# Another beginning, another end of the output projection and another entry of the feed-forward part in a one-core hybrid decoder layer

## The chip, the cores and the metric

The kernel runs on one core of a Trainium2 chip. A core has five engines that work side by side, each through its own list of instructions in order: PE (TensorE, matrix products), DVE (VectorE), ACT (ScalarE), POOL (GpSimd) and SP (SyncE, which here only starts transfers). An instruction waits on semaphores until its inputs are there and its output buffer is free; whatever stands behind it on its engine waits too. Matrix products read SBUF and write PSUM. The metric is the time in microseconds (us) of one execution on the device, taken as the median of several runs.

## The reference, cut to what matters

One decoder layer works on 512 prompt rows and 8 sample rows, 520 columns in all once the activations are transposed:

```python
sh1, sc1, g1, sh2, sc2, g2 = ada_mod(c, w_ada, b_ada)         # silu(c) @ w_ada + b_ada, six vectors
h = modulate(rmsnorm(x, norm1_w), sh1, sc1)                   # rmsnorm(x) * (1 + sc1) + sh1
mq, mk, ..., ga, gb = jnp.split(h @ w_in + b_in, SPLIT_POINTS, axis=-1)
...
merged = jax.nn.sigmoid(ga) * (y_m @ w_proj_a) + jax.nn.sigmoid(gb) * (y_f @ w_proj_b)
x = x + g1 * (merged @ w_out)
h2 = modulate(rmsnorm(x, norm2_w), sh2, sc2)
f_out, conv_new = conv_ffn(h2, conv_state, w_ffn_in, conv_w, conv_b, w_ffn_out)
x = x + g2 * f_out
```

`D_MODEL` is 2048, `D_FF` 5632, everything is float32. Between `split` and `merged` stand a matrix memory and an attention, which the change does not touch.

## The kernel before, in words

**Products.** Every float32 product is made of three products of a faster type: a weight tile is cast to `wh` on ACT and its remainder `wl` is formed on DVE; an activation is split in the same way into a high and a low part; PE forms `wh`·high, `wh`·low and `wl`·high. 2048 rows of activations are 16 chunks of 128 rows (`KC` = 16), the 520 columns are two halves `z` of 260 (`HN`). Weights come in raw tiles of 512 KB through SP; there are eight raw buffers, two sets of `wh`/`wl`, and a third one (`cf`) from the output projection on.

**The beginning.** The class `First` computes the first layer's shift and scale for two chunks at a time (a phase; `phases` has eight): it loads pieces of `w_ada` of 256 KB (`ar`), PE multiplies them (`adp`), ACT copies the sums (`ads`), PE transposes them (`adq`), DVE adds the bias (`ada`). Then the two chunks are modulated (`x`), split (`hh`, `hl`), and multiplied with two chunks' worth of eleven outputs of `w_in` (`NPRE`, tiles `pre`); the partial sums of the eleven outputs are kept, so that each phase adds to them. `load_group` loads these weights, in groups of four, four and three outputs. In the text the groups are numbered from g0, so g3 is the first group of phase 1. `next_group`, at outputs 1, 4 and 8 of a phase, loads one further group and splits the next one. At two visits per phase, `v0` and `v1`, PE does the next phase's `adp` products; at `v1 + 1` the next phase's `finish` and modulation follow. PSUM has two buffers for `pre`, so output j waits until the copy or the addition of output j − 2 is done. From the first phase on PE, DVE and ACT work in the order in which the code is written (`Ordered`).

**The output projection.** `merged @ w_out` runs as eight units (`WoPair`, two chunks of output each) of seven products, in the manner of Strassen; `run_pairs` gives each product a slot t (56 in all), and before it issues the preparations for later ones: `total` (sums of weight tiles), `split`, and `take`, which moves a finished product out of PSUM. The first unit has the order `ORDER1`, the others `ORDER`. A dictionary `late` hangs further work on single slots. Each finished output row chunk is stored (`dx2`), squared, added up for the next norm (by a transfer that accumulates on POOL), scaled and stored (`dxa`), except for the last pair, whose chunks are squared here and enter the norm directly (`half_squares`, `half_norm`).

**The entry of the feed-forward part.** `half_norm(z)` sums the squares on PE (`ms`) and `rsqrt` turns them into the factor of the norm (`rr`) on ACT and DVE. `features` makes the split activations (`bf`) of eight chunks and one half from the scaled rows `xa`. PE uses them at once: `fa`, `fg` and `fb` are the accumulators of the first columns; `beside` runs several weights over one set of activations, `eight` one weight. `cast` and `low` prepare `wh` and `wl`. Afterwards the regular units (`FfnPair`) begin.

Of the kernel before, what the change touches and what calls it, by code (L numbers as in the profile page):

```python
# [63 lines left out]
def tile_hybrid_step(ctx: ExitStack, tc: tile.TileContext, I, O):  # L64
# [191 lines left out]
    class Pair:  # L256
# [82 lines left out]
    def run_pairs(units, early, late, start=None):  # L339
        loads = {2: {1: ((0, 0),), 2: ((1, 0), (1, 1)), 5: ((0, 1),)},  # L340
                 1: {1: ((0, 0),), 3: ((1, 0), (1, 1)), 5: ((0, 1),)}}[early]
        for t in range(-early if start is None else start, 7 * len(units) + 5):
            u, r = divmod(t, 7)
            now, nxt = (units[v] if 0 <= v < len(units) else None for v in (u, u + 1))
            if 0 <= u - 1 < len(units):
                units[u - 1].after(r + 7)
            if now:
                if r > 0:
                    now.take(now.order[r - 1])
                now.ahead(r)  # L350
            if nxt:
                if r in loads and now:
                    nxt.load(*loads[r])
                if r >= 7 - early:
                    nxt.ahead(r - 7)
            if t in late:
                late[t]()
            if now:
                now.product(now.order[r])
# [92 lines left out]
    class First:  # L452
# [42 lines left out]

        def finish(self, c0, n):
            t = ada_turn(ada_out(self.ps, n), n)
# [10 lines left out]
        def steps(self, c0, n):  # L508
            return [lambda s=s: self.part(c0, n, s) for s in range(KC // 2)] + [lambda: self.finish(c0, n)]
# [31 lines left out]
    def modulate_first(u, c, eng):  # L541

        a, b = SC1 * 16 + c, SH1 * 16 + c
        V.tensor_scalar(u[:, :SEQ], u[:, :SEQ], ada[:, a, 0:1], ada[:, b, 0:1], op0=ALU.mult, op1=ALU.add)
        V.tensor_tensor(u[:, SEQ:N], u[:, SEQ:N], ada[:, a, 1:9], op=ALU.mult)
        V.tensor_tensor(u[:, SEQ:N], u[:, SEQ:N], ada[:, b, 1:9], op=ALU.add)
        return split(hp, "hl", u, "h", eng=eng)

# [24 lines left out]

    load_group()
    first.load(NPH)
    for _ in range(3):
        load_group()
# [7 lines left out]
    w_first = wtwo([raws.pop(0)[0]], m * NPH * P)  # L585
    h = []
# [7 lines left out]
    def first_chunks(c0, n):  # L594
        for c in range(c0, c0 + n):
            h.append(modulate_first(xs[c], c, V))

    normed(*phases[0])
    first.finish(*phases[0])
    first_chunks(*phases[0])  # L600
# [27 lines left out]
    T, V, S = (Ordered(tc, e) for e in (T, V, S))  # L628
    for i, (c0, n) in enumerate(phases):
        todo = {1: [next_group], 4: [next_group], 8: [next_group]}  # L630
        visits, steps = {}, []
        if i + 1 < len(phases):
            a, b = range(c0 + n, c0 + 2 * n)
            steps = first.steps(c0 + n, n)
            v0, v1 = {0: (3, 7), 1: (3, 6)}.get(i, (1, 4))
            visits = {v0: 4, v1: 4}
            for j, f, c in ((0, norm_x, a), (2, norm_x, b), (v1 + 1, mod_x, a), (v1 + 2, mod_x, b), (9, mod_low, a),
                            (10, mod_low, b)):
                todo.setdefault(j, []).append(on(f, c))
            todo[v1 + 1].append(on(mod_high, a))  # L640
            todo[v1 + 2].append(on(mod_high, b))
        for j in range(NPRE):
# [11 lines left out]
            for k in range(n):  # L654
                o = (j % m * n + k) * P
                for e, (a, b) in enumerate(((wh, h[c0 + k][0]), (wh, h[c0 + k][1]), (wl, h[c0 + k][0]))):
                    for z in range(2):
                        T.matmul(acc[:, z, :HN], a[:, o:o + P], b[:, z * HN:(z + 1) * HN],
                                 start=(k == 0 and e == 0), stop=(k == n - 1 and e == 2))
# [8 lines left out]
    xs = wh = wl = None  # L668
# [943 lines left out]
    class WoPair(AddPair):  # L1612
# [9 lines left out]
        def ahead(self, r):  # L1622
            super().ahead(r)
            if r == 0:
                self.fetch(lambda c: I["xT"][:, c, :])

        def done(self, e):
# [3 lines left out]
            if c == KC - 2 + e:  # L1631
                return
# [15 lines left out]
        def after(self, r):  # L1648
            if r > 8 or self.c == KC - 2:
                return  # L1650
            if r == 7:
                self.add(1, 0, self.x)
                self.done(0)
# [4 lines left out]
        def end(self, step):  # L1658

            if step == 0:  # L1660
                self.add(1, 0, self.x)
            if step == 1:
                super().c11()
                self.done(0)
                self.done(1)
# [86 lines left out]
    W2 = units[-1]  # L1752
# [11 lines left out]
    def half_squares(z):  # L1764
        a, b = z * HN, (z + 1) * HN
        if z:
            W2.sq = [pt("sq") for _ in range(2)]
        for e in range(2):
            S.activation(W2.sq[e][:, a:b], W2.x2[e][:, a:b], AF.Square)
# [10 lines left out]

    def first_weights(o):
        ws.append(parts2(0, o, 0))
        load2(1, o, 0)

    r2 = st("rr")
    run_pairs(units, 2, {
        0: lambda: (m_sums(7, 0), m_sums(7, 1), m_parts(7, 6)), 1: lambda: (m_parts(7, 5), m_sums(7, 2)),
# [564 lines left out]
```

## Time and profile before

| what | value |
|---|---|
| time, median of 3 runs | 2893.94 us (2893.7 to 2894.21) |
| the profiled execution's own time | 2878.36 us |
| its span in the trace | 2876.6 us |
| PE busy | 2836.9 us, 99% |
| weight loads (overlap PE) | 2728.6 us |
| DVE busy | 2153.9 us, 75% |
| ACT busy | 1367.4 us, 48% |
| POOL busy | 361.3 us, 13% |
| mean granted TensorE clock | 0.999 |
| bytes moved | 514.16 MB, mean 179 GB/s |

Read it thus: PE is busy nearly throughout, so a change of order can only win time where PE stands idle; and the other engines count where PE waits for them. The profiled execution is 15.6 us shorter than the median of the runs, so differences found in the profile are carried over to the median as differences. The rows themselves stand in the prediction.

### The profile page before, as it was taken

How to read it: one execution, taken by the hardware profiler on the slowest of the kernel's cores; microseconds unless marked ns; L12 is line 12 of the kernel's file. 1: busy time of each engine (PE TensorE's matmuls, PEld its weight loads, DVE VectorE, ACT ScalarE, POOL GpSimd, SP SyncE). 2: the span in 40 equal slices, each digit the busy share in tenths (PEclk: the TensorE clock that was granted, in tenths of full speed). 3: DMA queues.
4: the chain of work that ended last, by engine and by line, in shares of the span. 5: the costliest groups of instructions: out<-in, count | busy, mean ns of one | idle time of the engine just before them, and what ended most of it. 6: DMA issues, size and time to landing. Idle time of an engine off the chain costs nothing.

```text
span 2876.6 us, 58533 instructions
## 1 busy us (share of the span) xinstructions
PE 2836.9 (99%) x23460; PEld 2728.6 (95%) x23460; DVE 2153.9 (75%) x3992; ACT 1367.4 (48%) x2395; POOL 361.3 (13%) x649
## 2 busy tenths in 40 slices
PE   6999999999999999999999999999999999999999
PEld 4889998999998889899999999999999999999999
DVE  5777755677864566468888888888888887787787
ACT  4235643455554555334555444444454445544543
POOL 0001111211110112502211000000000001100100
PEclk9999999999999999999999999999999999999999
DMA  9934448844546576757763444444443436746752
GB/s 336 315 124 124 147 138 285 272 162 149 170 140 227 189 252 228 261 184 228 218 212 97 129 142 140 145 136 152 139 147 118 145 113 201 191 154 187 205 159 89
DMA packets 214138, 514.16 MB, mean 179 GB/s; under 512 B 24480, under 2 KB 77072, under 8 KB 213864
## 3 DMA queue, kind: packets, MB, share of 16 engines
q1 hardware_dynamic: 177072, 416.01, 45.0%
q0 software_dynamic: 36352, 94.18, 10.9%
q8 instruction: 184, 3.01, 0.4%
q14 instruction: 90, 0.74, 0.1%
q10 hardware_dynamic: 440, 0.23, 0.0%
HBM read 440.40 MB, written 66.46 MB: 176 GB/s over the span
## 4 chain that ended last, share of the span: by engine, by line
PE 85%; DVE 5%; issue 4%; DMA 3%; ACT 2%; POOL 0%; SPq 0%; ACTq 0%; POOLq 0%; DVEq 0%
PE x L60 31%; PE y L60 15%; PE z L60 8%; PE fi L223 7%; PE pre L60 4%; PE pa L223 3%; PE fo L60 3%; PE gate L223 3%; PE mo L223 2%; PE adp L428 2%; PE adp L60 1%; PE mv L223 1%; DMA ar<-in_w_ada 1%; DVE wl L60 1%; PE mk L223 1%
## 5 line engine op out<-in xcount | busy, mean ns | idle before, releaser
L60 ACT CAST wh<-sw 128x512 fp32r<-128x512 f32 x638 | 365.7, 621 | 245.6 <-PE z L60 75.8
L60 DVE TENSOR_TENSOR wl<-sw,wh 128x512 fp32r<-128x512 f32 x638 | 411.3, 686 | 87.0 <-ACT wh L60 84.2
L60 PE MATMUL x<-bf,wh 128*128 128x260 f32 x2624 | 476.2, 282 | 0.2 <-DVE tg L60 0.2
L60 ACT CAST wh<-raw 128x1024 fp32r<-128x1024 f32 (+2 forms) x349 | 315.7, 917 | 327.6 <-PE x L60 130.7
L60 DVE TENSOR_TENSOR wl<-raw,wh 128x1024 fp32r<-128x1024 f32 (+2 forms) x349 | 364.9, 1057 | 121.9 <-ACT wh L60 113.8
L60 PEld LDWEIGHTS x<-bf,wh 128*128 128x128 f32 x2624 | 403.4, 188 | 0.4 <-issue 0.4
L60 PE MATMUL x<-bf,wl 128*128 128x260 f32 x1312 | 369.6, 282 | 0.0
L178 DVE TENSOR_TENSOR wl<-raw,wh 128x1024 fp32r<-128x1024 f32 (+1 forms) x116 | 140.7, 1213 | 194.5 <-ACT wh L177 192.5
L60 PEld LDWEIGHTS x<-bf,wl 128*128 128x128 f32 x1312 | 247.0, 188 | 0.0
L60 PE MATMUL y<-bf,wh 128*128 128x260 f32 x1312 | 238.6, 282 | 0.0
L177 ACT CAST wh<-raw 128x1024 fp32r<-128x1024 f32 (+1 forms) x116 | 120.5, 1039 | 204.1 <-issue 46.6
L60 DVE TENSOR_TENSOR sw<-raw,raw 128x512 f32<-128x512 f32 x316 | 203.0, 683 | 0.0
L60 PEld LDWEIGHTS y<-bf,wh 128*128 128x128 f32 x1312 | 201.7, 188 | 0.0
L60 PE MATMUL x<-ff,wh 128*128 128x260 f32 x1024 | 185.9, 282 | 0.0
L60 PE MATMUL y<-bf,wl 128*128 128x260 f32 x656 | 184.8, 282 | 0.0
L60 PEld LDWEIGHTS x<-ff,wh 128*128 128x128 f32 x1024 | 157.6, 188 | 0.0
L60 PE MATMUL x<-ff,wl 128*128 128x260 f32 x512 | 144.5, 282 | 0.0
L60 PE MATMUL x<-hf,wh 128*128 128x260 f32 x720 | 131.0, 282 | 0.0
L60 PE MATMUL fo<-fe,wh 128*128 128x260 f32 x768 | 125.6, 284 | 1.2 <-DVE fo L60 1.1
L60 PEld LDWEIGHTS y<-bf,wl 128*128 128x128 f32 x656 | 123.5, 188 | 0.0
L60 PE MATMUL z<-bf,wh 128*128 128x260 f32 x656 | 120.6, 284 | 0.0
L60 PEld LDWEIGHTS x<-hf,wh 128*128 128x128 f32 x720 | 110.6, 188 | 0.0
(620 smaller groups left out, 7543.8 us busy)
## 6 DMA issues: line engine op xcount, KB each, us to landing
raw<-in_w_fi SPq DMA_DIRECT2D x176, 512.0 KB, 4.4
raw<-in_w_in SPq DMA_DIRECT2D x156, 512.0 KB, 4.6
ar<-in_w_ada SPq DMA_DIRECT2D x192, 256.0 KB, 6.3
raw<-in_w_ada SPq DMA_DIRECT2D x96, 512.0 KB, 4.2
raw<-in_w_fo SPq DMA_DIRECT2D x64, 512.0 KB, 4.0
raw<-in_w_out SPq DMA_DIRECT2D x32, 512.0 KB, 4.7
raw<-in_w_fo SPq DMA_DIRECT2D x32, 384.0 KB, 3.7
dff<-cc POOLq DMA_DIRECT2D x44, 260.0 KB, 4.3
```

Source lines behind the costliest of these rows:

```text
L60: return lambda *a, **k: self.tc.keep_in_program_order(getattr(self.eng, op)(*a, **k))
L177: S.copy(wh[:, o], t[:, :m])
L178: V.tensor_tensor(wl[:, o], t[:, :m], wh[:, o].bitcast(F32), op=ALU.subtract)
L223: T.matmul(acc[:, z, :HN], a[:, o], b[:, z * HN:(z + 1) * HN], start=(k == 0 and i == 0), stop=(k == K - 1 and i == 2))
L428: ins = T.matmul(ps[32 * g:32 * g + 32, :], cs[:, k, :], w, start=first, stop=last, tile_position=(0, 32 * g))
```

## The change: what it does

It has four parts.

1. *Beginning.* The loads start in another order: first all of phase 0's `ar`, then g0 and g1, four pairs of phase 1's `ar`, g2, then the remaining `ar` as far as buffers allow. g3 is no longer loaded ahead but by the first `next_group`. The first two chunks' high parts are written by ACT straight from `x` with scale and shift; DVE forms the modulated value afterwards for the low part. The first weight is split in two pieces, and phase 0's products are ordered by kind. The copy of the `adp` sums (`sums`) is separated from `finish` and done one output earlier. In phase 0 `v0` is 4 instead of 3. Modulation and high parts of both next chunks stand ahead of `next_group`.
2. *First unit of the output projection.* `m_parts(7, 6)` moves from slot 0 to slot 1, and there the split of the next weight comes ahead of `total(3)`.
3. *Last two units.* `run_pairs` takes a table of places; with `tail` the last two units share slots 40 to 55: their long products come one unit after the other, then the next-to-last unit's last two, then the last unit's last two. The last two pairs (four chunks) are no longer squared, accumulated and stored by transfers; all four are squared into tiles of their own for the norm, so that `half_norm` has four products with `ones` instead of two. Half of the norm and the first four features stand in slots 52 to 55.
4. *Entry.* The norm of the other half comes after all eight features instead of after four, one weight's products over half 0 are merged with those of two others, the scaling of the last rows moves, and `sums_of` lets a weight's `wl` be formed ahead of its last step.

On SP the loads of the beginning before stand thus (`ar` are pieces of `w_ada`, `raw` a group of `w_in`; the fourth `raw` of the program, raw38, is g3):

```order
L478 DMA ar35_182<-in_w_ada 128x2x256
L570 DMA raw36_184<-in_w_in 128x4x256
L570 DMA raw37_186<-in_w_in 128x3x256
L570 DMA raw38_188<-in_w_in 128x4x256
L478 DMA ar39_190<-in_w_ada 128x2x256
```

And after, further down the same queue, behind g0, g1, g2, all `ar` of phase 1 and part of phase 2's (raw100 is g3):

```order
L492 DMA ar94_370<-in_w_ada 128x2x256
L492 DMA ar95_372<-in_w_ada 128x2x256
L579 DMA raw100_394<-in_w_in 128x4x256
L492 DMA ar110_463<-in_w_ada 128x2x256
L492 DMA ar111_465<-in_w_ada 128x2x256
```

g3 was row 37 of SP, ahead of phase 1's `ar`, and is now row 63, in the place that g4 had (row 64).

On ACT at the end of phase 0 before (ads132 are the sums of phase 1, wh135 is the cast of g3, hh137 and hh143 are phase 1's high parts, the `pre` are copies of outputs 8 to 10):

```order
L60 COPY ads132_565<-adp106_427 128x256
L60 CAST wh135_578<-raw38_188 128x1024
L60 CAST hh137_585<-x4_91 128x520
L60 COPY pre140_601<-pre139_588 128x520
L60 CAST hh143_611<-x5_93 128x520
L60 COPY pre146_627<-pre145_614 128x520
L60 COPY pre148_643<-pre147_630 128x520
```

And after (hh135 and hh137 are the high parts, wh140 the cast of g3, pre143 the copy of output 8):

```order
L60 COPY ads125_542<-adp109_446 128x256
L60 COPY pre133_569<-pre132_556 128x520
L60 CAST hh135_583<-x4_91 128x520
L60 CAST hh137_589<-x5_93 128x520
L60 CAST wh140_594<-raw100_394 128x1024
L60 COPY pre143_611<-pre142_598 128x520
L60 COPY pre147_631<-pre146_618 128x520
L60 COPY pre149_647<-pre148_634 128x520
```

The cast of g3 now stands behind both high parts and ahead of the copies of the last three outputs.

On ACT in the first unit of the output projection before (mf2419 is the high part that `m_parts(7, 6)` makes, tt2423 the first product taken out of PSUM):

```order
L60 CAST wh2415_16227<-sw2392_16178 128x512
L60 CAST wh2415_16227<-sw2393_16180 128x512
L60 CAST mf2419_16240<-sgm2239_15011 128x260
L60 COPY tt2423_16270<-x2420_16243 128x260
L60 CAST wh2426_16276<-sw2390_16174 128x512
```

And after (tt2426 and mf2427 are the same two):

```order
L60 CAST wh2419_16237<-sw2394_16184 128x512
L60 CAST wh2419_16237<-sw2395_16186 128x512
L60 COPY tt2426_16277<-x2423_16250 128x260
L60 CAST mf2427_16279<-sgm2241_15017 128x260
L60 CAST wh2428_16282<-sw2392_16180 128x512
```

The copy and the cast have changed places.

The diff, cut to its core:

```diff
         def ahead(self, r):
+            swap = r == 1 and self.order == ORDER1
+            if swap:
+                self.split(self.order[r + self.early])
             if self.early == 2:
...
-            if r + self.early < 7:
+            if r + self.early < 7 and not swap:
                 self.split(self.order[r + self.early])
...
+        if tail:
+            place[-2][5:] = [end - 4, end - 3]
+            place[-1] = [end - 9, end - 8, end - 7, end - 6, end - 5, end - 2, end - 1]
...
+    first.load(NPH)
+    for _ in range(2):
+        load_group()
+    first.load(KC, 4)
     load_group()
-    first.load(NPH)
-    for _ in range(3):
-        load_group()
     first.load()
...
+    for c in range(NPH):
+        S.activation(h[c][0][:, :SEQ], xs[c][:, :SEQ], AF.Identity, scale=col_of(SC1, c), bias=col_of(SH1, c))
...
-            v0, v1 = {0: (3, 7), 1: (3, 6)}.get(i, (1, 4))
-            visits = {v0: 4, v1: 4}
...
+            v0, v1 = {0: (4, 7), 1: (3, 6)}.get(i, (1, 4))
+            visits = {v0: 4, v1: 5}
+            for j, f, c in ((min(v1 + 2, 8), mod_x, b), (v1 + 1, mod_x, a)):
+                todo.setdefault(j, [])[:0] = [on(f, c), on(mod_high, c)]
...
+            if self.c == KC - 4:
+                return
...
+        def ahead(self, r):
+            if r == 1 and not self.c:
+                m_parts(7, 6)
+            super().ahead(r)
...
+        def end(self):
+            super().c11()
+            for u in units[-2:]:
+                for e in range(2):
+                    G.dma_start(dx2[u.c + e], u.x2[e][:, :N])
...
-        for i, (w, t) in enumerate(((onesr, W2.tot[0]), (onesr, W2.tot[1]), (ones, W2.sq[0]), (ones, W2.sq[1]))):
-            T.matmul(ps, w, t[:, a:b], start=(i == 0), stop=(i == 3))
+        parts = [(onesr, t) for t in W2.tot] + [(ones, t) for t in W2.sq]
+        for i, (w, t) in enumerate(parts):
+            T.matmul(ps, w, t[:, a:b], start=(i == 0), stop=(i == len(parts) - 1))
...
     run_pairs(units, 2, {
-        0: lambda: (m_sums(7, 0), m_sums(7, 1), m_parts(7, 6)), 1: lambda: (m_parts(7, 5), m_sums(7, 2)),
...
+        0: lambda: (m_sums(7, 0), m_sums(7, 1)), 1: lambda: (m_parts(7, 5), m_sums(7, 2)),
...
+        52: lambda: half_squares(1), 53: lambda: half_norm(1), 54: entry_a, 55: entry_b}, 0, True)
...
-    beside(some, 0, 1, range(4))
+    beside(some, 0, 1)
     half_norm(0)
...
     eight(1, 0, 0, (1,), ws[2])
     features(0, 0)
-    beside(some, 0, 0)
-    eight(1, 0, 0, (0,), ws[2])
...
+    beside(some + [(1, 0, ws[2])], 0, 0)
...
-    sums_of(4, 5)
-    w0 = low2(casts.pop())
+    sums_of(4, 5, between=lambda: low(ws))
+    w0 = ws.pop()
```

More of the change, by code (lines that the diff above doesn't have):

```diff
@@ L508, in steps @@
         def steps(self, c0, n):
-            return [lambda s=s: self.part(c0, n, s) for s in range(KC // 2)] + [lambda: self.finish(c0, n)]
+            return [lambda s=s: self.part(c0, n, s) for s in range(KC // 2)] + [lambda: self.sums(n), lambda: self.finish(c0, n)]
     def ada_steps(which):
@@ L1620, in x2_tile @@
             return st("x2")
[L1622 to L1625, printed above, removed]
         def done(self, e):
@@ L1847, in features, with cast, low, entry_a @@
+            if j >= 2:
+                feature_low(e * 8 + j - 2, z)
             if j in between:
                 between[j]()
+    casts, some = [], []
+    def cast(*x):
+        casts.append(cast2(*x))
+    def low(out):
+        out.append(low2(casts.pop()))
+    def entry_a():
+        cast(0, 0, 0)
+        load2(1, 0, 0)
+        for i in range(3):
+            feature(i, 1)
+        feature_low(0, 1)
+        feature_low(1, 1)
+        low(ws)
+    def entry_b():
+        cast(0, 1, 0)
+        load2(1, 1, 0)
+        half_squares(0, (0, 1))
+        feature(3, 1)
+        low(ws)
+        feature_low(2, 1)
@@ L1978, in tile_hybrid_step @@
     load2(2, 1, 1)
-    sums_of(6, 7)
-    w0 = low2(casts.pop())
+    sums_of(6, 7, between=lambda: low(ws))
+    w0 = ws.pop()
     eight(2, 1, 0, (1, 0), w0)
```

202 lines of the change are left out of this document (111 added, 91 removed).

## The prediction

> **What bounds the kernel now.** I read the page's busy shares first, then the PE waits of the three stretches that the diff touches, then the rows around each wait.
>
> ```profile
> span 2876.6 us, 58533 instructions
> PE 2836.9 (99%) x23460; PEld 2728.6 (95%) x23460; DVE 2153.9 (75%) x3992; ACT 1367.4 (48%) x2395; POOL 361.3 (13%) x649
> ```
>
> PE is the bound: 2876.6 − 2836.9 = 39.7 us is all that it stands idle. The change removes no product, so it can only win from these 39.7 us. Where they lie (columns: what PE waited for, us in total, times, longest), beginning, first unit of the output projection, and entry of the feed-forward part:
>
> ```profile
> PE adp L428 <- DMA ar<-in_w_ada: 17.8, 1, 17.8
> PE pre L60 <- ACT hh L234: 2.7, 1, 2.7
> PE pre L60 <- DVE pre L60: 1.9, 1, 1.9
> PE pre L60 <- ACT pre L60: 1.2, 1, 1.2
> PE adq L60 <- ACT ads L60: 1.0, 1, 1.0
> PE x L60 <- ACT tt L60: 1.8, 1, 1.8
> PE fa L60 <- DVE bf L60: 1.4, 3, 0.6
> PE fa L60 <- ACT bf L60: 1.1, 1, 1.1
> PE fa L60 <- DVE wl L60: 0.5, 1, 0.5
> PE fg L60 <- DVE wl L60: 0.2, 1, 0.2
> ```
>
> The 17.8 us until the first `w_ada` pieces land stay: the first eight loads are the same. The rest that the edits can reach is 2.7 + 1.9 + 1.2 + 1.0 + 1.8 + 1.4 + 1.1 + 0.5 + 0.2 = 11.8 us, 0.4% of the time. That, and a little that the rows below add, is the ceiling of any gain.
>
> **The beginning.** The rows ahead of the first product, those at the end of phase 0, and the loads:
>
> ```profile
> 33.01 0.55 DVE L544 TENSOR_SCALAR x<-x,ada 128x512 f32<-128x512 f32 x1
> 34.20 1.15 ACT L234 CAST hh<-x 128x520 fp32r<-128x520 f32 x2 [2.62 <-DVE x L546]
> 34.88 0.80 PE L60 MATMUL pre<-hh,wh 128*128 128x260 f32 x2 [2.75 <-ACT hh L234]
> 53.95 1.06 ACT L60 CAST wh<-raw 128x1024 fp32r<-128x1024 f32 x1
> 58.00 0.58 ACT L60 COPY pre<-pre 128x520 f32<-128x520 f32 x1
> 27.49 22.14 SPq L478 DMA_DIRECT2D ar<-in_w_ada  x26
> 50.01 0.37 SPq L570 DMA_DIRECT2D raw<-in_w_in  x1
> raw<-in_w_in SPq DMA_DIRECT2D x1, 512.0 KB, 6.7
> 32.00:34.00 2.00, 0.13 (x2) 0.00 (x0) 1.76 (x9) 0.00 (x0) 0.00 (x0) 0.76 1.09 349
> 38.00:40.00 2.00, 2.00 (x11) 2.00 (x11) 0.25 (x1) 1.54 (x2) 0.00 (x0) 0.53 1.10 348
> 40.00:42.00 2.00, 2.00 (x20) 1.80 (x22) 1.59 (x2) 0.71 (x2) 0.00 (x0) 1.00 1.09 346
> ```
>
> The last three are windows: stretch, its length, busy PE, PEld, DVE, ACT and POOL with their instructions, granted TensorE clock, DMA share, GB/s. The transfers run at about 349 GB/s without a gap, so a load's landing time is set by the bytes ahead of it.
>
> *Start of phase 0.* One 512 KB group now stands behind phase 0's `ar` instead of among them: 512 KB at 349 GB/s is 1.5 us, so the sums come 1.5 us sooner. Then ACT writes the first high part straight from `x`: the 1.2 us from DVE's modulation (33.01) to ACT's cast (34.20) leave the path. Together the first product starts about 2.7 us sooner, near 32.15.
>
> *End of phase 0.* g3 gives this back in part. The order shows it in the place of the load that was issued at 50.01 and needed 6.7 us, so landed at 56.7; ahead of it is one 512 KB load less, so I expect it at 56.7 − 1.5 = 55.2. ACT is strictly in order: behind the cast of g3 (1.06) stands the copy of output 8 (0.58), and output 10 needs that PSUM buffer. 55.2 + 1.06 + 0.58 gives 56.9, against 58.6 now (58.00 + 0.58). Since PE, 2.7 us early and without the waits of 1.0 and 1.2 us, is through with output 9 at about 53.4, it idles some 3.5 us there, and of all that only 58.6 − 56.9 = 1.7 us is won. In phase 1 the casts of both high parts now stand ahead of the weight cast (0.6 us each, by the two at 34.20), which lengthens the 1.9 us wait by about 0.6 and spares about 0.3 elsewhere: 1.7 − 0.6 + 0.3 = 1.4 us won, if the clock stays. Later groups land some 6 us ahead of use and cost nothing; if they were as late as g3, each would cost its lateness one for one.
>
> *The clock.* After the 2.75 us idle from 32.1 the granted clock fell: 0.76 over 32 to 34, 0.53 over 38 to 40, 1.00 from 40 on. That fits one half clock over 1 of the 2 us from 32 on and until 39.9. Pairs of products had 0.43 between starts in that state, against 0.24 after:
>
> ```profile
> 38.81 0.64 PE L60 MATMUL pre<-hh,wl 128*128 128x260 f32 x2
> 39.24 0.64 PE L60 MATMUL pre<-hh,wh 128*128 128x260 f32 x2
> 40.25 0.40 PE L60 MATMUL pre<-hh,wh 128*128 128x260 f32 x2
> 40.49 0.40 PE L60 MATMUL pre<-hl,wh 128*128 128x260 f32 x2
> ```
>
> From 34.88 to 39.9 these are 11.5 pairs, by 0.19 each 2.2 us lost. The new idle of 3.5 us is longer, but follows full work, and the waits of 1.9 and 1.2 us left no lower clock behind. So the cost lies between 0 and 2.2; I take the middle, 1.1, since rows speak for both. The old loss at 34.88 to 39.9 may vanish or not, and matters nothing as long as g3 sets the end of the phase. Beginning: −1.4 + 1.1 = **−0.3 us** (from −2.1 to +1.5).
>
> [...]
>
> **First unit of the output projection.**
>
> ```profile
> 1330.82 0.41 ACT L60 CAST mf<-sgm 128x260 fp32r<-128x260 f32 x1 [2.19 <-DVE sgm L60]
> 1331.13 0.37 ACT L60 COPY tt<-x 128x260 f32<-128x260 f32 x1
> 1331.56 0.51 PE L60 MATMUL x<-mf,wh 128*128 128x260 f32 x2 [1.81 <-ACT tt L60]
> ```
>
> The copy `tt` frees the PSUM tile for the third product, and waits behind a cast that waits 2.19 us for DVE. With the two exchanged the copy runs at once: 1.81 less some 0.1 us. The cast moved behind it (0.41), and the DVE remainder after it, are needed only two products later, and `total(3)`, put behind the split, three products later; a late weight could take some of it back. **−1.7 us** (from −1.8 to 0).
>
> **Tail and entry.**
>
> ```profile
> 1484.57 1.04 PE L60 MATMUL ms<-sq,ones 128*128 128x260 f32 x4
> 1489.62 0.39 PE L60 MATMUL fa<-bf,wh 128*128 128x260 f32 x1 [1.14 <-ACT bf L60]
> 1494.33 0.28 PE L60 MATMUL ms<-hi,onesr 128*128 128x260 f32 x1
> 1495.26 0.47 PE L60 MATMUL fa<-bf,wh 128*128 128x260 f32 x1
> 1499.18 0.40 PE L60 MATMUL fb<-bf,wh 128*128 128x260 f32 x2
> 1497.52 0.46 ACT L60 ACTIVATE rr<-ms,eps 128x260 f32<-128x260 f32 x1
> 1500.88 0.48 DVE L60 SCALAR_TENSOR_TENSOR bf<-xa,ada,bf 128x260 fp32r<-128x260 f32 x1
> 1507.95 1.03 ACT L60 CAST wh<-raw 128x1024 fp32r<-128x1024 f32 x1
> 1509.02 1.23 DVE L60 TENSOR_TENSOR wl<-raw,wh 128x1024 fp32r<-128x1024 f32 x1
> 1517.38 0.39 PE L60 MATMUL fg<-bf,wl 128*128 128x260 f32 x1 [0.23 <-DVE wl L60]
> ```
>
> - More work on PE: the four `ones` instructions of a half take 0.86 us by their starts (a fourth of it each); there are eight now, so +0.86 for each half, +1.7.
> - The features of the first half: 24 products by 0.12 (half of the 0.24 of a pair above) are 2.9 us, yet from 1489.62 to 1494.33 the first 24 took 4.7 and from 1495.26 to 1499.18 the next 24 took 3.9; with the wait of 1.14 ahead that is 1.8 + 1.0 + 1.1 = 4.0 us lost. The norm now has three products behind it instead of one (2.9 us each), and four features are made by then: −4.0. The first `fg` must wait for the last product's addition on DVE to free its PSUM tile, about +0.4 (0.48 is the DVE row of that shape above).
> - The other half's norm comes after all eight features. From its logarithm (1497.52) to the end of the first low part (1500.88 + 0.48) are 3.84 us, and only one set of 2.9 us stands beside them now; before, four features did too. +1.0.
> - The merged products use the first weight (`wh` of 0,0,0) nearly to their end. The weight that takes its buffer, now cast at 1507.95 beside another 2.9 us of products, can be cast only then: 1.03 + 1.23 less the 0.7 us of products that no longer need it, +1.6. The next two casts shift along, so that the 0.23 wait becomes about 0.8, +0.6.
> - `between` forms a `wl` ahead of two additions on DVE, some 0.8 us sooner: the 0.5 wait goes, −0.5.
> - Two `dxa` stores, two accumulating transfers and two loads less, four `dx2` stores later on POOL: hidden, nobody on PE's path waits for them; if `xa` were late, its features would be.
> - Interleaving the two units leaves the products the same. In slots 46 and 47 DVE has more additions than before, some 2 us by my count of the order; weights split two slots ahead (5.7 us of products) absorb it, or PE waits up to that.
>
> 1.7 − 4.0 + 0.4 + 1.0 + 1.6 + 0.6 − 0.5 = **+0.8 us** (from −2.4, if the stalls of 1.0, 1.6 and 0.6 are covered, to +2.8, if DVE falls behind in the interleaved slots).
>
> **Sum.** −0.3 − 1.7 + 0.8 = −1.2 us: 2878.36 becomes 2877.2 in the profiled execution, which is 15.6 under the median. Carried to the median: 2893.94 − 1.2 = 2892.7. A difference under 0.2% (5.8 us), about what a measurement of this kernel can tell from no change, I call the same.
>
> **Rivals.**
> *All waits are won.* If g3 lands before about 50.7, the copies do not wait and the beginning wins 2.7 + 1.0 + 1.2 + 0.6 = 5.5; with 1.8 and a covered entry (−2.4) that is −9.7: 2884.2. The unbroken 349 GB/s and g3's place in the queue speak against it.
> *Slower, by g3.* The 26 `ar` issues took 22.14 us, 0.85 each where 256 KB at 349 GB/s are 0.75: SP is held up at times by buffers that PE frees, covered by the 6.7 us of transfers under way. PE now frees the first of phase 1's one output later (`v0` is 4). Should this let the transfers run dry, g3 comes later and PE waits one for one. From a landing at 56.4 on, 1.2 later than I expect, the kernel is slower than before; at 60 it takes 2897.5, from 62.2 on it is over 0.2% slower. For it speaks that nothing else covers g3; against it that the transfers show no gap now.
> *The clock at its full price.* With the rows' 2.2 us the sum is −0.1: 2893.8.
>
> **How the numbers follow.** The forecast, within 2.5 us of its number, 0.53; the clock 0.18; all won 0.13; slower by g3 0.16, of which 0.07 lies beyond 0.2%. Faster by over 0.2% (under 2888.1) comes from the first rival, 0.12 of its 0.13; slower from the second, 0.07, and 0.02 for an interleaving worse than bounded; the rest, 0.79, is the same. The forecast's own range is 2890.2 to 2895.2. The bounds of the terms add up to −2.1 − 1.8 − 2.4 = −6.3 and +1.5 + 0 + 2.8 = +4.3, that is 2887.6 to 2898.2; I take the lower end 1 us lower, 2886.6, since the losses at the features were larger than their listed waits and others may be too. All won lies below this range, the far half of g3 above.
>
> **What would show it.** Right: the first `pre` near 32 and no 2.7 us wait for `hh`; a PE wait of 3 to 4 us between 53 and 57 that goes back to a cast whose raw tile landed near 55; no wait on `tt`; waits of 1 to 2 us on `bf` and `wl` where 1497 to 1517 was. Wrong: g3 there before 51 or after 57, no low clock or a long one behind it, or long waits in slots 42 to 55.

## The result: 0.16% slower

The changed kernel takes 2900.05 us (median of 22 runs), the kernel before on the same chip 2894.53 us (22 runs). The ratio is 1.0016 with a 95% interval of 1.001 to 1.0022, that is +4.6 us (2.9 to 6.4); the medians are 5.5 us apart. The forecast was −1.2 us and a range of 2886.6 to 2898.2: the sign and the range were wrong.

The profiled execution of the changed kernel, the page's head and the waits of PE over the whole span (what PE waited for, us in total, times, longest):

```profile
span 2900.3 us, 58539 instructions
PE 2850.7 (98%) x23468; PEld 2740.1 (94%) x23468; DVE 2155.6 (74%) x3993; ACT 1367.5 (47%) x2400; POOL 361.0 (12%) x645
...
PE adp L442 <- DMA ar<-in_w_ada: 17.2, 1, 17.2
PE gate L223 <- issue: 7.9, 15, 1.1
PE pre L60 <- DVE pre L60: 5.2, 7, 2.5
PE pre L60 <- ACT pre L60: 3.1, 1, 3.1
PE pre L60 <- ACT hh L60: 2.2, 2, 1.9
...
PE fb L60 <- DVE wl L60: 0.8, 1, 0.8
PE fg L60 <- DVE wl L60: 0.7, 1, 0.7
PE fa L60 <- ACT bf L60: 0.6, 1, 0.6
...
PE y L60 <- ACT tt L60: 0.5, 1, 0.5
...
PE fg L60 <- DVE x L60: 0.3, 1, 0.3
PE fb L60 <- ACT wh L60: 0.3, 1, 0.3
```

The span is 23.7 us longer than that of the kernel before in its profile, some five times what the ratio gives. Most of that, 18.0 us, lies between the first `mo` and the output projection, where the code of both kernels is the same: there stands the row `gate <- issue`, 7.9 us in which PE waits for nothing that the profile shows, with a low clock behind it (0.59 over 1164 to 1174 us, 0.73 over 1174 to 1184). The experiments below find the same row in the kernel before, so it does not come with the change. The chips differ: in three of the five comparisons below and here the kernel before takes 2880 us, in the others 2890 and 2894.

The other rows fit the steps of the prediction, except for one: `pre <- DVE pre` occurs seven times instead of twice. To see what each stage costs, I cut each trace at the first start of certain products. For each pair of marks the table gives the time from one to the other, in us:

| kernel | first `adp` to `mo` (the phases) | first product of the output projection to its third accumulator `z` | to the first `fa` (rest of the projection) | to the first regular unit (entry) | to `fo` (41 units) |
|---|---|---|---|---|---|
| before, first profile | 185.20 | 16.60 | 149.31 | 74.48 | 844.44 |
| after, first profile | 188.71 | 15.28 | 148.68 | 75.74 | 847.79 |

By these, the beginning costs 3.5 us, the first unit wins 1.3, tail and entry together cost 0.6, and 3.4 us are lost in the regular units, which the change does not touch. The five columns, which leave out the stretch with `gate`, add up to +6.2 us; part of it is chance in one execution, and the runs with the parts alone separate it.

### The profile page after: what moved, and what is told of

Its sections match the earlier page's. It is cut to its first block, busy times and chain, and to the rows that moved or that the text cites. A ratio compares the mean times of both kernels' runs of the same rounds, so it can differ in the third digit from the quotient of the medians.

```text
span 2900.3 us, 58539 instructions
## 1 busy us (share of the span) xinstructions
PE 2850.7 (98%) x23468; PEld 2740.1 (94%) x23468; DVE 2155.6 (74%) x3993; ACT 1367.5 (47%) x2400; POOL 361.0 (12%) x645
## 4 chain that ended last, share of the span: by engine, by line
PE 87%; issue 4%; DVE 3%; ACT 1%; DMA 1%; POOL 0%; SPq 0%; ACTq 0%; POOLq 0%; DVEq 0%
PE x L60 31%; PE y L60 16%; PE z L60 8%; PE fi L223 7%; PE gate L223 4%; PE fo L60 4%; PE pa L223 3%; PE pre L60 2%; PE mo L223 2%; PE adp L442 2%; PE mv L223 1%; PE adp L60 1%; PE fg L60 1%; PE fa L60 1%; DMA ar<-in_w_ada 1%
## 5 line engine op out<-in xcount | busy, mean ns | idle before, releaser
L60 DVE TENSOR_TENSOR wl<-raw,wh 128x1024 fp32r<-128x1024 f32 (+3 forms) x351 | 366.5, 1055 | 130.1 <-ACT wh L60 123.1
L60 ACT CAST wh<-raw 128x1024 fp32r<-128x1024 f32 (+3 forms) x351 | 317.0, 915 | 298.1 <-PE x L60 132.8
```

The lines of the kernel that those rows point to most:

```text
L60: return lambda *a, **k: self.tc.keep_in_program_order(getattr(self.eng, op)(*a, **k))
```

## Experiments

### The four first: one part alone

The kernel before against itself, unchanged:

> The kernel before, unchanged, against itself. Theory (the stall of PE on its own instructions in the gate stage, 7.9 us by the waits of the changed kernel, and the spread of about 10 us among runs belong to single executions, not to the change): ratio 1.000 within 0.05%, and a profile of this kernel can show waits of PE for 'issue' in the gate stage, or a span 10 to 20 us over the 2876.6 of the first profile. Rival (the stall comes with the changed kernel's instruction stream): no such wait here and a span near 2877.

Measured: 2879.1 against 2880.14 us, ratio 0.9995 (0.9986 to 1.0004). On this chip there is no wait for issue. That is what the rival says too; the kernel before on another chip decides it further down. An effect under 0.1% is not separated from none by one such comparison; the traces have to say which stage it is in.

Only the beginning:

> Only the beginning of the change, the rest as before. Theory (the beginning loses: 0.45 us in each of phases 2 to 7 and two low clocks of about 1.3 us each, in all +2.9 us at the end of the phases): slower by 2.5 to 3.5 us, 0.1%, with waits of PE for the addition of pre on DVE in phases 2 to 7. Rival (the beginning is neutral, the loss lies in the gate stage): within 1 us.

```diff
-    load_group()
     first.load(NPH)
-    for _ in range(3):
+    for _ in range(2):
         load_group()
+    first.load(KC, 4)
+    load_group()
     first.load()
...
-            visits = {v0: 4, v1: 4}
+            visits = {v0: 4, v1: 5}
...
+            for j, f, c in ((min(v1 + 2, 8), mod_x, b), (v1 + 1, mod_x, a)):
+                todo.setdefault(j, [])[:0] = [on(f, c), on(mod_high, c)]
```

Measured: 2882.97 us, ratio 1.0012 (1.0003 to 1.0021): +2.8 us by the medians, which are 2.83 apart. The waits of PE from phase 2 on, 80 to 205 us:

```profile
PE pre L60 <- DVE pre L60: 5.2, 7, 2.5
```

One is the 2.5 us wait of phase 1, and one of 0.33 at the very end stands in the kernel before too. The other five are new, 0.45 to 0.53 in each of phases 2 to 6, 2.4 in all (phase 7 has no next phase to prepare; the expectation counted six). Their cause stands in the changed kernel's rows of ACT, DVE and PE in phase 2 (start, duration, instruction, in brackets the idle time before and its releaser):

```profile
93.60 0.37 ACT L60 COPY ads<-adp 128x256 f32<-128x256 f32 x1 [9.17 <-PE adp L60]
93.87 0.84 ACT L60 CAST wh<-raw 128x768 fp32r<-128x768 f32 x1
...
94.74 0.96 DVE L60 TENSOR_TENSOR wl<-raw,wh 128x768 fp32r<-128x768 f32 x1 [2.41 <-ACT wh L60]
95.61 0.69 DVE L60 TENSOR_TENSOR pre<-pre,pre 128x520 f32<-128x520 f32 x1
...
98.72 0.51 PE L60 MATMUL pre<-hh,wh 128*128 128x260 f32 x2 [0.53 <-DVE pre L60]
```

and of the kernel before, ACT and DVE in the same phase:

```profile
90.64 0.83 ACT L60 CAST wh<-raw 128x768 fp32r<-128x768 f32 x1 [6.76 <-PE pre L60]
92.75 0.37 ACT L60 COPY ads<-adp 128x256 f32<-128x256 f32 x1 [1.28 <-PE adp L60]
...
91.50 0.96 DVE L60 TENSOR_TENSOR wl<-raw,wh 128x768 fp32r<-128x768 f32 x1
94.33 0.70 DVE L60 TENSOR_TENSOR pre<-pre,pre 128x520 f32<-128x520 f32 x1 [1.87 <-PE pre L60]
```

The copy of the sums (`ads`) now stands at output 4, ahead of that output's weight cast. Ahead of it ACT is idle for 9.17 us, until PE's `adp` products are done, and the cast, which before stood ahead of the copy and started at 90.64, now starts behind it at 93.87. `wl` comes at 94.74 instead of 91.50, falls among the additions of `pre` and the next chunks' modulation on DVE, and PE waits half a microsecond for a PSUM buffer. Phases 2 to 6 take 21.1 to 21.2 us each instead of 20.7: 2.1 us in all.

Only the first unit of the output projection:

> Only the edits in the first unit of the output projection. Theory: the wait for tt of 1.8 us goes, one of 0.5 us on the next product comes, 1.4 us faster, 0.05%. Rival (the gain is lost later to DVE): no difference, with a new wait before the end of that unit.

```diff
+            if r == 1 and not self.c:
+                m_parts(7, 6)
             super().ahead(r)
...
+            swap = r == 1 and self.order == ORDER1
+            if swap:
+                self.split(self.order[r + self.early])
...
-        0: lambda: (m_sums(7, 0), m_sums(7, 1), m_parts(7, 6)),
+        0: lambda: (m_sums(7, 0), m_sums(7, 1)),
```

Measured: 2878.19 us, ratio 0.9992 (0.9983 to 1.0001), 1.95 us less by the medians; the interval just reaches no change, so the trace has to carry it. In its trace the wait of 1.8 us is gone and one of 0.5 is there instead:

```profile
PE y L60 <- ACT tt L60: 0.5, 1, 0.5
```

Only tail and entry (the change without what the two runs above have, `m_parts(7, 6)` in slot 0 as before):

> Only the interleaved last two units and the rewritten entry. Theory: +0.8 us, 0.03%, made of 4 us less waiting for the first features and of new waits of about 0.6 (bf), 1.0 (wh and wl of fb) and 0.7 (wl of fg). Rival (tail and entry cost what the whole kernel lost): +3 to +5 us.

```diff
+        if tail:
+            place[-2][5:] = [end - 4, end - 3]
+            place[-1] = [end - 9, end - 8, end - 7, end - 6, end - 5, end - 2, end - 1]
...
+        0: lambda: (m_sums(7, 0), m_sums(7, 1), m_parts(7, 6)),
...
-    beside(some, 0, 0)
-    eight(1, 0, 0, (0,), ws[2])
+    beside(some + [(1, 0, ws[2])], 0, 0)
```

Measured: 2882.26 us, ratio 1.0008 (0.9999 to 1.0017), 2.1 us more by the medians, and again the interval just reaches no change. Its waits in the entry are the expected ones:

```profile
PE fb L60 <- DVE wl L60: 0.8, 1, 0.8
PE fg L60 <- DVE wl L60: 0.7, 1, 0.7
PE fa L60 <- ACT bf L60: 0.6, 1, 0.6
PE fg L60 <- DVE x L60: 0.3, 1, 0.3
PE fb L60 <- ACT wh L60: 0.3, 1, 0.3
```

From `z` to the first regular unit it takes 148.82 + 75.76 = 224.58 us, 0.8 more than 149.31 + 74.48: the term that was forecast. But the 41 units after it take 846.67, against 844.30 in the kernel before on the same chip. The three parts add up to 2.8 − 1.95 + 2.1 = +3 us, at the lower end of the interval of the whole (2.9 to 6.4).

### Which edit of the beginning, and which of the entry

The beginning with the sums back in their old place from phase 2 on:

> Only the beginning, but in phases 2 to 7 the copy of the adp sums stands again where it stood before the change, one output later, behind the weight cast. Theory (that copy waits for PE and holds the weight cast behind it on ACT, so that wl and the additions of pre on DVE come late): the six waits of about 0.45 us for pre in phases 2 to 7 go, 2.5 us less than the beginning alone, that is +0.3 us against the kernel before. Rival (the waits come from the modulation that was put ahead, or from PE's order in these phases): the six waits stay and the time is that of the beginning alone, +2.8 us.

```diff
-            visits = {v0: 4, v1: 5}
+            visits = {v0: 4, v1: 4 if i > 1 else 5}
...
-            if visits and j == v1 + 1:
-                steps.pop()()
+            while steps and j == v1 + 1:
+                steps.pop(0)()
```

Measured: 2881.36 against 2880.04 us, ratio 1.0003 (0.9994 to 1.0012). The five new waits are gone; from 80 to 205 us the trace has

```profile
PE pre L60 <- DVE pre L60: 2.9, 2, 2.5
```

so the theory holds for them: 5.2 − 2.9 = 2.3 us, and the phases take 20.7 us again. The time itself, +1.3 us by the medians where +0.3 was expected, is too coarse to add to this.

The same with g3 early:

> As the run before, and g3 is loaded right behind g2, ahead of the remaining pieces of w_ada. Theory (g3 is late by the 1.1 us that ACT waits for its raw tile; the other 2 us of the 3.1 us wait come from ACT's order: both high parts, the cast, and only then the copy of output 8): the wait at the end of phase 0 shrinks from 3.1 to about 2.0 us, the clock may hold, 1 to 2 us faster than the run before: -1 us against the kernel before. The prediction's rival (all waits are won once g3 is early): the wait goes wholly, -4 us or more.

```diff
     first.load(KC, 4)
     load_group()
+    load_group()
     first.load()
```

Measured: 2879.92 us, ratio 0.9998 (0.9989 to 1.0007), 1.4 us less than the run before, as expected; level with the kernel before, where −1 us was expected. ACT at the end of phase 0, first in the changed kernel, then in this one:

```profile
51.88 1.36 ACT L60 CAST hh<-x 128x520 fp32r<-128x520 f32 x2 [1.50 <-DVE x L60]
54.36 1.04 ACT L60 CAST wh<-raw 128x1024 fp32r<-128x1024 f32 x1 [1.13 <-DMA raw<-in_w_in]
55.31 1.08 ACT L60 COPY pre<-pre 128x520 f32<-128x520 f32 x2
```

```profile
53.18 1.36 ACT L60 CAST hh<-x 128x520 fp32r<-128x520 f32 x2 [1.50 <-DVE x L60]
54.45 1.04 ACT L60 CAST wh<-raw 128x1024 fp32r<-128x1024 f32 x1
55.40 1.08 ACT L60 COPY pre<-pre 128x520 f32<-128x520 f32 x2
```

With g3 in time the cast starts behind the high parts at once, and PE's wait falls from 3.1 to 1.9 us, not to nothing. The lateness of g3 is 1.1 us of it; the rest is the order on ACT: the copy of output 8, which could have run at 51.4, stands behind two high parts that wait for DVE and behind the cast. The clock, which was to hold, fell behind this wait too in the profiled execution (0.66 over 56 to 60 us).

The tail with the third weight's products apart:

> Only the tail and the entry, but the third weight's products over half 0 stand again by themselves behind the two others. Theory (merging kept the first weight's buffer in use to the end, so that the next cast came late): the waits of 0.3 and 0.75 us on fb and the one of 0.7 us on fg go or fall to 0.2, 1.5 us less than tail and entry alone, about -0.6 us by the profile against the kernel before. Rival (the casts are late because of ACT's own order): the waits stay.

```diff
-    beside(some + [(1, 0, ws[2])], 0, 0)
+    beside(some, 0, 0)
+    eight(1, 0, 0, (0,), ws[2])
```

Measured: 2881.91 us, ratio 1.0004 (0.9995 to 1.0013): 1.9 us slower than the kernel before by the medians, where −0.6 was expected, and by the interval not separated from no change. The waits of its entry:

```profile
PE fg L60 <- DVE wl L60: 0.6, 1, 0.6
PE fa L60 <- ACT bf L60: 0.6, 1, 0.6
PE fg L60 <- DVE x L60: 0.4, 1, 0.4
```

Both waits on `fb` are gone, so they did come from the buffer that merging kept in use; the one on `fg` fell only by 0.1. From `z` to the first regular unit: 148.83 + 74.16 = 222.99 us, 0.8 better than before the change, as expected. What is missing lies behind: the 41 units take 846.32.

All of this put together, with the beginning's order on ACT mended:

> The changed kernel with the sums copied as before in phases 2 to 7, g3 loaded early, in phases 0 and 1 both modulations first on DVE, then the weight cast, and the high parts behind the copy of output 8, and the third weight's products apart. Theory: the wait at the end of phase 0 and its low clock go (-4 to -5 us at the start of phase 1), the wait in phase 1 goes (-1.9), first unit -1.4, tail -0.6: 6 to 8 us faster than the kernel before, 0.2 to 0.3%. Rival (pieces of w_ada come late instead, because g3 takes 1.5 us of the transfers ahead of them): new waits of adp for ar of 1 to 2 us each and not more than 4 us faster.

```diff
-            for j, f, c in ((min(v1 + 2, 8), mod_x, b), (v1 + 1, mod_x, a)):
-                todo.setdefault(j, [])[:0] = [on(f, c), on(mod_high, c)]
+            if i < 2:
+                todo.setdefault(v1 + 1, [])[:0] = [on(mod_x, a), on(mod_x, b)]
+                todo[9] = [on(mod_high, a), on(mod_high, b)]
+            else:
+                for j, c in ((v1 + 1, a), (v1 + 2, b)):
+                    todo.setdefault(j, []).extend([on(mod_x, c), on(mod_high, c)])
```

Measured: 2874.48 against 2880.04 us, ratio 0.998 (0.9971 to 0.9989), 5.6 us faster, a little short of the 6 to 8 expected. The wait at the end of phase 0 is gone, the one in phase 1 is 0.8; the phases take 179.43 us instead of about 185. No `adp` waited more than 0.4 us for its pieces, so g3's earlier place cost nothing. The 41 units take 847.97.

### The whole kernel on another chip, and what lies behind the tail

The changed kernel and the kernel before once more:

> The changed kernel, unchanged. Theory (its loss is the sum of its parts, as measured one by one: beginning +2.8, first unit -1.9, tail, entry and what follows +2.1): +3.0 us on this chip too, and waits for 'issue' in the gate stage only if the kernel before shows them on this chip as well. Rival (the 7.9 us of issue waits in its first profile belong to this kernel): they come again, and it is 6 us or more slower.

> The kernel before once more, to see whether this chip shows waits of PE for issue in the gate stage without any change. Theory (they belong to a chip or an execution): with a median near 2894 they are there, with one near 2880 they are not. Rival (they belong to the changed kernel): not there in either case.

Measured: the changed kernel 2893.66 against 2889.94 us, ratio 1.0013 (1.0004 to 1.0022), 3.7 us slower; the kernel before against itself 1.0 (0.999 to 1.0009). This chip is one with the longer time, and here the unchanged kernel has, in its own trace:

```profile
PE gate L223 <- issue: 6.8, 12, 1.0
```

and the changed one 5.2 us in ten. The rival falls: the wait comes with the chip, or what runs on it, and not with the change.

One tile more ahead of the feed-forward activations of the kernel before:

> The kernel before with one tile of SBUF more, taken ahead of the feed-forward activations and cleared in two columns by POOL, so that the activation tiles behind it lie in other places; no product, no order on PE changes. Theory (the feed-forward units run at a slightly different pace because the tiles lie elsewhere, which would explain the 2 us that all kernels with the new tail lose between the first regular unit and fo): the time of that stage differs from 844.2 us by 0.5 us or more. Rival (the pace follows from the order of the tail, or from what it leaves late): 844 to 844.5 us as in all kernels with the old tail.

```diff
     X = {n: [None] * 8 for n in range(1, 8)}
     hb = {}
+    spare = st("spare")
+    G.memset(spare[:, 0:2], 0.0)
+    spare = None
```

Measured: 2890.23 us, ratio 1.0002 (0.9991 to 1.0013). The 41 units take 844.42 in all, as with the old tail: by its own mark the theory fails here. Yet the single units changed. Without `adp` products a unit takes 20.10, 20.13 or 20.05 us in turn in the kernel before, and 20.10, 20.12, 20.14 with the spare tile; no wait is listed in either. These times belong to the program: in the three profiles of the kernel before, from at least two chips, they agree to 0.01 us. Together with units with `adp` that came out shorter, the sum stayed.

To follow this, the new tail with one and with two spare tiles:

> The new tail and entry alone, with one more tile taken from the ring of SBUF tiles ahead of the feed-forward activations, cleared in two columns by POOL. Theory (places): the stage from the first regular unit to fo moves from 846.7 by 0.5 us or more, and the three unit times 20.13, 20.09, 20.18 change. Rival (order of the tail): 846.3 to 847.0 with the same unit times.

> As the run before with two more tiles. Theory (places): another time of that stage, other unit times than with none or one. Rival: as with none.

```diff
     hb = {}
+    spare = [st("spare") for _ in range(2)]
+    for t in spare:
+        G.memset(t[:, 0:2], 0.0)
+    spare = t = None
```

Measured by one profile each (2883.41 and 2883.52 us, the kernel before 2879.93 there): the 41 units take 846.67 with one and 845.39 with two, against 846.67 with none. The plain units: 20.13, 20.09, 20.18 with none, 20.10, 20.11, 20.13 with one, 20.13, 20.09, 20.17 with two. And the units with `adp` products move: the one of 23.45 us with none (22.05 in the kernel before) is 22.05 with one and 22.08 with two, while another, 22.18 with none, is 23.99 with one. The long unit is no accident of one execution: in all six profiles of the new tail without a spare tile that unit takes 22.9 to 23.6 us. In it, PE waits for a piece of `w_ada`; the tail alone, then the kernel before at the same place:

```profile
2241.61 1.92 PE L60 MATMUL adp<-ar,cs 128*32 128x512 f32 x14
2243.86 1.05 PE L60 MATMUL adp<-ar,cs 128*32 128x512 f32 x2 [0.34 <-DMA ar<-in_w_ada]
2244.84 0.39 PE L60 MATMUL z<-bf,wh 128*128 128x260 f32 x1
```

```profile
2239.65 1.92 PE L60 MATMUL adp<-ar,cs 128*32 128x512 f32 x16
2241.50 0.39 PE L60 MATMUL z<-bf,wh 128*128 128x260 f32 x1
```

So the loss behind the tail has two pieces. One is which of the `adp` pieces comes late, 1.4 and 1.8 us in the two seen, and this moves when the ring of tiles is shifted. The other is the pace of plain units, 20.13 on average instead of 20.09; it moved with one spare tile and not with two. That shifting the ring moves or removes the first piece is shown, by one execution for each shift. Whether it is the place of the tiles or the earlier tile whose release a load must wait for is not separated, and that the new tail loses by this is likely rather than shown: the same shift cost the old tail nothing (844.42). For the second piece two shifts are too few to name a cause, and with two spare tiles 0.8 us still remain over the 844.6 that the old tail has on average.

### The improved kernel, with the old tail and with the new one

> The improved beginning (sums as before in phases 2 to 7, g3 early, modulations first and high parts behind the copy of output 8) and the first unit's edits, with the old tail and entry. Theory (the tail costs 2 us in what follows it and wins 0.3 with the weights apart): 5.5 to 7.5 us faster than the kernel before, 1 to 2 us better than the best kernel so far. Rival (the tail's gain is real and what follows is chance): 1 to 2 us behind it.

Its edits are those of the run called the best above, without the hunks on `run_pairs`' places, `WoPair`'s end and everything behind it:

```diff
-    run_pairs(units, 2, {
...
-        52: lambda: half_squares(1), 53: lambda: half_norm(1), 54: entry_a, 55: entry_b}, 0, True)
+    run_pairs(units, 2, {
+        0: lambda: (m_sums(7, 0), m_sums(7, 1)), 1: lambda: (m_parts(7, 5), m_sums(7, 2)),
...
+        54: lambda: (first_weights(0), half_squares(1)), 55: lambda: (first_weights(1), half_norm(1))}, 0)
```

Measured on the chip with the longer time: 2880.87 against 2889.94 us, ratio 0.9971 (0.996 to 0.9981), 8.4 us faster by the ratio and so somewhat more than the 5.5 to 7.5 expected.

Both side by side on one chip:

> The improved beginning and the first unit's edits with the old tail, once more. Theory (the new tail loses 2 us over all): 6 to 8 us faster than before, 1 to 2 us ahead of the next run. Rival (the 8 to 9 us on the chip before were luck): 5 to 6 us, level with the next run.

> The same with the new tail and entry, the third weight's products apart. Theory: 5 to 6 us faster than before. Rival: level with the run before.

Measured: with the old tail 2871.52 against 2879.93 us, ratio 0.9968 (0.9956 to 0.998), 8.4 us faster by the medians; with the new tail 2873.9 us, 0.9974 (0.9963 to 0.9985). The two are 2.4 us apart, a little more than the 1 to 2 foreseen, but their intervals overlap; that the old tail is better rests on the traces. By the traces the new tail is 0.7 us better up to the first regular unit (148.52 + 74.16 against 148.95 + 74.47) and 3.3 us worse in the 41 units (847.85 against 844.54). The waits of the version with the old tail in the first 205 us, which answer to those of the kernel before:

```profile
PE adp L431 <- ACT sq L392: 18.2, 1, 18.2
PE pre L60 <- ACT hh L60: 2.2, 2, 1.9
PE pre L60 <- DVE pre L60: 1.1, 2, 0.8
PE adq L60 <- ACT ads L437: 0.6, 1, 0.6
PE pre L60 <- DVE hl L60: 0.5, 1, 0.5
PE ms L408 <- DVE hi L399: 0.4, 1, 0.4
```

Of the change, then, the beginning is worth keeping once three places in it are mended, and the first unit's exchange is worth keeping as it is.

## Why the prediction was wrong, step by step

- *Ceiling and bound.* Right: PE is the bound, and what was won was idle time of PE and low clock behind such time (over 56 to 60 us the clock was 0.57 in the changed kernel and 1.00 in the run called the best).
- *Start of phase 0* (first product 2.7 us sooner, near 32.15): right. It starts at 31.91, 14.71 us after the first `adp` instead of 17.06: 2.3 us by that mark. A wait of 1.9 us for `hh` is left there.
- *End of phase 0* (g3 at 55.2, a wait of 3.5 us): right in size, 3.12 us, with g3's cast at 54.36. The split was wrong: the first rival held that with an early g3 all waits would be won, yet with g3 early 1.9 us remained.
- *The later phases.* This is the step that failed. The prediction followed the moved copies only through phases 0 and 1; of the later ones it said only that their groups land in time and cost nothing, and so took the separate copy of the sums at nothing there. It brings a wait of 0.45 to 0.53 us in each of five, 2.4 in all, and makes these phases 2.1 us longer: the raw tile is there, but its cast now stands behind a copy that waits for PE.
- *The clock* (0 to 2.2 us, 1.1 taken): after the wait at the end of phase 0 it fell in all four executions that have g3 late (over 56 to 60 us 0.57 in three, 0.62 with the sums back), so the rival was right that it falls. The price lies between: 1.5 us, by the two places where executions with and without a fall can be compared (see the last section). Up to the start of phase 2 the change cost 0.2 us on average, where −0.3 was forecast; the later phases cost the rest. The phases as a whole cost 2.1 us on average over three executions with the changed beginning (188.71, 187.41, 187.37) against nine with the old one (184.54 to 187.46, mean 185.7).
- *First unit* (−1.7): right in size, in part by luck; −1.95 by the runs, and 15.26 instead of 17.1 us on average in the traces. The exchange alone won 1.3 us, since a wait of 0.5 us on `tt` came at the next product, which the forecast did not have; the rest is a low clock that the old wait left behind in some executions (0.50 over 1332 to 1334 us in the kernel before run again, 1.00 in its first profile), which it did not have either.
- *Tail and entry* (+0.8): right as a sum, 0.6 to 0.8 us by the traces, and the waits came where they were foreseen. Each was shorter: 0.35, 0.57, 1.05 and 0.5 us for the terms of 0.4, 1.0, 1.6 and 0.6, together 1.1 us less. So, with the 1.7 us of more work as forecast, about 1 us less than the 4.0 was won at the features; that the two cancel is luck. The buffer of the merged weight is shown to be the cause of the two on `fb`.
- *Behind the entry.* Second failure: the sum ended at the entry, so the units behind it were put at nothing without a word. The 41 units after it took 845.4 to 848.0 us in the eight executions profiled with the new tail (two of them with spare tiles), and 844.0 to 845.3 in the ten without it, on average 847.0 against 844.6: +2.4. The changed kernel itself took 847.6 and 847.8, the kernel before 844.3 to 844.4: +3.3. The cause is open.
- *Slower, by g3.* The rival on the other side named the wrong place: g3 came 0.8 us sooner than forecast, not later.

With the measured terms, +2.1 − 1.9 + 0.7 + 2.4 = +3.3 us, or +4.2 with the 3.3 of the kernel's own units, against +3.7 and +4.6 us in the two comparisons of the whole kernel. Both lie within the intervals of the two.

## What to carry to other kernels

An operation that is split off and issued earlier waits earlier too, and on an engine that works in order everything behind it waits along (here a cast started at 93.87 us instead of 90.64): look at each phase of a loop in which it lands, not only at the one for which it was moved. When a profile shows an early load as the cause of a wait, ask what stands between the load's consumer and the instruction that PE needs; here two thirds of the wait were the order on ACT, and the load moved alone won a third of it. And compare stages that nobody touched: a change that takes other tiles can move loads there (here a unit took 23.45 us, and 22.05 with one tile more).

## What the runs showed of the hardware that was not expected

- *Behind a wait of 1.9 us the clock was 0.50 in some executions and 1.00 in others.* In nine executions with the old beginning, PE waits 1.9 us at the same place in phase 1. In six the clock stayed at 1.00, in three it fell to 0.50 (over 82 to 84 us); the kernel with only the first unit's edits is one of the latter (stretch 82 to 84 us, clock before the last two columns), and the kernel before run again one of the former:

```profile
82.00:84.00 2.00, 2.00 (x12) 2.00 (x11) 1.39 (x3) 0.03 (x1) 0.00 (x0) 0.50 1.10 348
```

```profile
82.00:84.00 2.00, 2.00 (x26) 1.54 (x29) 1.86 (x4) 0.65 (x1) 0.00 (x0) 1.00 1.10 350
```

Phases 1 and 2 together took 44.9 us where it fell and 43.3 to 43.4 where it did not: a fall costs 1.5 us. (The whole phases differ by 2.5 us, 187.1 to 187.5 against 184.5 to 185.3; the rest of that lies in phase 0.) The same holds for the 1.8 us wait in the first unit of the output projection: 16.6 us in seven executions, 18.1 in four, again 1.5 apart. So removing that wait won 1.3 us or 2.9, and the average of 1.9 is what the runs show.

  Where the wait lies may decide. In the first profiles of the two kernels the times at which the granted clock changes lie whole multiples of 3.41 us apart: in the changed kernel it is 0.50 over 32.51 to 35.92, over 56.41 to 59.82 and over 80.30 to 83.71, and 1.00 between these; in the kernel before it is 0.50 over 33.04 to 39.87, beginning within the wait of 2.75 us, and 1.00 behind that. In the 3.41 us ahead of these four falls PE is idle for 2.50, 2.96, 2.03 and 1.73 us. In the kernel before, the 1.9 us wait of phase 1 lasts from 79.39 to 81.28; 80.83 is twelve times 3.41 us behind 39.87, in the 3.41 us ahead of it PE is idle for 1.51 us and in those behind it for 0.45, and the clock stays at 1.00. That the place of the wait decides is the author's reading of these few cases; no condition for a fall is shown.

- *The old entry has a price that its waits do not show.* In two of the ten executions with the old entry the clock was 0.50 for 6.8 us within it (1505.2 to 1512.1 us in the kernel with one spare tile), and the entry took 75.8 and 75.9 us instead of 74.5. In the first profiles the clock is 1.00 throughout the entry, 74.48 us long before the change and 75.74 us after it.

- *PE can wait where the profile shows no cause.* PE waits in rows named 'issue' in the gate stage, 7.9 us in the changed kernel's first profile and 5.2 to 7.0 us in each of the four kernels profiled on the chip on which the kernel before takes 2889.94 us, in the stretch in which POOL gathers rows from the caches; the clock falls behind it (0.64 over 1160 to 1170 us in the kernel before), and the span is some 12 us longer (2889.2 against 2877.4 us in the kernel before on two chips). In the eight profiles on the two chips on which it takes 2880.14 and 2880.04 us no such row is listed. That PE lacks instructions there is a guess; what it waits for, and why the chips differ, is open.
